# Attention with single-buffered v: each v load issued in two parts by partitions, and the next head's v asked for one step later

## The chip, the core and the metric

The kernel runs on one core of one Trainium2 chip. The time is the device time of one execution in microseconds (us), the median of three runs. TensorE (PE) multiplies, VectorE (DVE), ScalarE (ACT) and GpSimd (POOL) work element by element, SyncE (SP) issues the transfers (DMAs), which 16 DMA engines carry out.

## The reference, cut to what matters

One layer of an encoder runs over two sequences of 272 and 1040 tokens (16 of them are prepended). A gated feed-forward half-step, then a mixer of four differential attention heads beside a pooling branch, a projection, a second feed-forward half-step and a final norm. The part that the change touches is the attention of one head:

```python
logits = jnp.einsum('bqhcd,bkhcd->bhcqk', q_blk, k).astype(jnp.float32) * scale
logits = logits + bias[None, :, None]
p = jax.nn.softmax(logits, axis=-1)
a = p[:, :, 0] - lam * p[:, :, 1]
return jnp.einsum('bhqk,bkhd->bqhd', a.astype(v.dtype), v)
```

followed by a norm of each output row. All data are float32.

## The kernel before, in words

**Products.** Each float32 operand is split into a high and a low part, and a product is made of three (`mm3`, lines 157 to 163): high x high (L161), low x high (L162), high x low (L163). So v is held as two tiles, `vh` and `vl`, and a product with v first needs `vh` (L161), then `vl` (L162).

**v in memory.** The projection before the attention writes q, k and v to DRAM tensors (`q_d`, `k_d`, `v_d`). `load_v(hd, q)` (lines 817 to 830) reads one head's v of one sequence (`q` is 0 for the 272 tokens, 1 for the 1040). Tokens lie on partitions in groups of `TK` = 92 or 116. Per part (high, low) there are two loads: a main one of all full groups (L826; 2 groups on 92 partitions, 92 KB, or 8 groups on 116 partitions, 464 KB) and a tail (L828; 88 partitions, 44 KB, or 112 partitions, 56 KB). Each run of consecutive bytes is one row of 128 floats, 512 B. That is four issues per head and sequence, 32 in all. The tiles have one buffer each (`bufs=1`): the next head's v can be loaded only when the last product with the old one is done.

**Steps.** There are 40 steps, 10 for each head: 2 blocks of 128 query rows of the short sequence, then 8 of the long one. `run(i)` (lines 978 to 995) writes, in this order: the logits of step i for the first map (L845, L846, evicted with the bias by DVE at L848, exponentiated by ACT at L863), the combination of step i-1 (`combine`: L872 on DVE; L875 and L876 on POOL for the long sequence), the work of `early[i]`, the transposes of step i-`LAG` (`LAG` = 3; L893, evicted by ACT and DVE as `at`), the logits of the second map, further transposes, and the work of `late[i]`. Products with v (`av`) are in `early`, three groups at a time, so those of one pair of long query blocks are spread over three steps; their norm (L223 to L229, L924, L242) and the write of `o` (L938) are in `late`.

**Loads.** They are put into `late` by hand (lines 947 to 974): k, bias and v of the next head, and q of the next pair of blocks in each even step, two issues (L791). With `s0` the first long step of head hd and `end` the step after its last, v of the long sequence of head hd+1 is written at `end + LAG + 1`, in a step numbered 14, 24 or 34; the last products with the old v are in `early` of the step after it (15, 25, 35), the first with the new v in `early[17]`, `early[27]` and `early[37]`. Before step 2, `load_v(0, 0)` and `load_v(0, 1)` load head 0's.

**Order of the queues.** All DMAs of this kernel are issued from SP, in order: an issue that waits holds up all behind it. The order in which each engine's instructions stand is not just the written one. The framework's planner takes the written order as priority and its own estimate of when each instruction is ready, and places it in its engine's queue; the queues are fixed when the kernel is built.

After the attention, lines 1209 to 1248 project its output; the `cat` loads (L807) bring the written outputs of heads and pooling groups back.

Of the kernel before, what the change touches and what calls it, by code (L numbers as in the profile page):

```python
# [11 lines left out]
F32 = mybir.dt.float32  # L12
# [48 lines left out]
LAG = 3  # L61
# [41 lines left out]
def encoder(ctx: ExitStack, tc: tile.TileContext, a: dict):  # L103
    nc = tc.nc
# [525 lines left out]
    rows = [[row[:, s : s + NS] for s in pair] for pair in places]  # L630
# [186 lines left out]
    def load_v(hd, q):  # L817
        nt = len(KT[q])
        m = TK[q]
        s = LENS[0] * q  # L820
        vv = []
        for t in range(2):
            v = qp.tile([m, nt, P], F32R, tag=f"v{t}{q}", name="v", bufs=1)
            src = v_d[t][:, hd * P : (hd + 1) * P]
            full = (nt - 1) * m
            nc.sync.dma_start(out=v[:, : nt - 1].bitcast(F32), in_=src[s : s + full].rearrange("(j p) d -> p j d", p=m))  # L826
            tail = KT[q][-1][1]
            nc.sync.dma_start(out=v[:tail, nt - 1].bitcast(F32), in_=src[s + full : s + full + tail])  # L828
            vv.append(v)
        state["v", hd, q] = vv  # L830
# [112 lines left out]
    def at(i, fn, *args):  # L943
        late[i].append((fn, args))

    per = len(QT[0]) + len(QT[1])
    for hd in range(HEADS - 1):
        s0 = per * hd + len(QT[0])
        end = s0 + len(QT[1])
        k_pool = ("pre", "qp")[(hd + 1) % 2]  # L950
        at(s0 + 1, load_k, "pre", hd + 1, 0)
        at(s0 + 1, load_bias, "pre", hd + 1, 0)
        at(s0 + 2, load_k, k_pool, hd + 1, 1)
        at(s0 + 4, load_bias, ("pre", "mp")[(hd + 1) % 2], hd + 1, 1)
        at(s0 + LAG + 3, load_v, hd + 1, 0)
        at(end + LAG + 1, load_v, hd + 1, 1)
    for s_ in steps:
        i = s_["n"]
        if s_["i"] == 0 and s_["si"] + 1 < len(supers):
# [1 line left out]
        if s_["i"] == SUPER - 1:  # L961
            nt = len(KT[s_["q"]])
            j = i + LAG
# [195 lines left out]
    with st:  # L1159
        load_v(0, 0)  # L1160
        load_v(0, 1)
        i = len(W_IN_LAST)
        while i < last_step + LAG or any(k >= i for k in early) or any(k >= i for k in late):
            run(i)
            i += 1
# [17 lines left out]
    rows = {}  # L1183
# [27 lines left out]
    for b in PAIRS2[0]:  # L1211
        s = BS2[b][0]
# [16 lines left out]
    for i, pair in enumerate(PAIRS2):  # L1229
# [5 lines left out]
        for m0 in range(0, KC, 2):  # L1235
            ws = [split_unit(raws[m]) if i == 0 and m < 2 else wcols(w_out, m) for m in (m0, m0 + 1)]
            for b in pair:
                s = BS2[b][0]
# [161 lines left out]
```

## Time and profile before

| | |
|---|---|
| median of 3 runs | 2452.47 us (2451.22 to 2454.18) |
| the profiled execution, own time | 2450.31 us |
| its span, first to last instruction | 2448.5 us |
| mean granted PE clock over the span | 0.979 of full speed |
| PE busy | 2336.4 us, 95% |
| DVE busy | 1506.1 us, 62% |
| ACT busy | 803.8 us, 33% |
| POOL busy | 387.6 us, 16% |
| transferred | 264.67 MB, mean 108 GB/s |

How to read it: busy shares are means over the whole span, while the attention steps that the change touches fill some 230 us of it, from about 1190 to 1422 us. There, what an engine waited for is read from the waits and the timeline. Times in the rows count from the span's start. A row of a timeline gives start and duration in us, and in brackets the idle time before it and what ended that. The granted clock is a share of full speed: 1.00 is 2.4 GHz, 0.50 is 1.2 GHz.

### The profile page before, as it was taken

What the parts mean: (1) busy time and instruction counts of PE and PEld (TensorE: products, weight loads), DVE (VectorE), ACT (ScalarE), POOL (GpSimd) and SP (SyncE); (2) the same over time, 40 slices, a digit from 0 to 9 for tenths busy, and PEclk for the clock granted to TensorE, in tenths of its full rate; (3) what the DMA queues carried; (4) which work ended last, traced back from release to release, by engine and by line L of the source; (5) the groups of instructions that cost most, each with busy time, mean ns of one, the idle gap of its engine ahead of it and who ended that gap; (6) DMA issues with size and microseconds to landing.
All of it is one profiled execution on the core that took longest, in us unless ns stands there. A gap on an engine that the chain in (4) does not pass through costs nothing.

```text
span 2448.5 us, 38316 instructions
## 1 busy us (share of the span) xinstructions
PE 2336.4 (95%) x14578; PEld 2181.6 (89%) x14578; DVE 1506.1 (62%) x2834; ACT 803.8 (33%) x1705; POOL 387.6 (16%) x479
## 2 busy tenths in 40 slices
PE   5999999999999998999888898899999999999998
PEld 5899999999888887889778898889999999988886
DVE  7964545448676667344477747685455446667665
ACT  6533333335011123111377723453333334211113
POOL 0000000000111124111376743100000000021112
PEclk7999999999999999999999998999999999999999
DMA  8422222245232224545754154432122216323222
GB/s 234 118 80 72 65 64 75 70 150 174 77 96 79 82 71 134 167 145 159 186 134 124 49 166 154 133 96 74 57 80 73 74 57 222 116 82 96 86 69 86
DMA packets 294591, 264.67 MB, mean 108 GB/s; under 512 B 22048, under 2 KB 254072, under 8 KB 293896
## 3 DMA queue, kind: packets, MB, share of 16 engines
q1 hardware_dynamic: 294408, 262.24, 35.3%
q8 instruction: 114, 1.87, 0.3%
q14 instruction: 69, 0.57, 0.1%
HBM read 190.79 MB, written 75.61 MB: 109 GB/s over the span
## 4 chain that ended last, share of the span: by engine, by line
PE 82%; DVE 8%; DMA 4%; POOL 2%; issue 2%; ACT 1%; SPq 1%; POOLq 0%; ACTq 0%; DVEq 0%
PE bank L162 26%; PE bank L161 26%; PE bank L163 26%; DVE wl L152 1%; DMA v<-v_d 1%; PE bank L893 1%; PE pair L845 1%; PE pair L846 1%; PE bank L242 1%; DMA wraw<-in_ffn_w_up 1%; DMA wraw<-in_ffn_w_gate 1%; DMA cat<-cat_d 1%; POOL l L876 0%; POOL ry L223 0%; DVE h L328 0%
## 5 line engine op out<-in xcount | busy, mean ns | idle before, releaser
L152 DVE TENSOR_TENSOR wl<-wraw,wh 128x512 fp32r<-128x512 f32 x320 | 235.3, 740 | 296.1 <-ACT wh L146 219.8
L530 DVE SCALAR_TENSOR_TENSOR h<-bank,h 128x272 f32<-128x272 f32 (+2 forms) x528 | 313.1, 601 | 155.3 <-PE bank L163 151.3
L161 PE MATMUL bank<-hl,wh 128*128 128x512 f32 (+2 forms) x1056 | 380.4, 360 | 0.0
L162 PE MATMUL bank<-hl,wl 128*128 128x512 f32 (+2 forms) x1056 | 379.4, 359 | 0.0
L163 PE MATMUL bank<-hl,wh 128*128 128x512 f32 (+2 forms) x1056 | 379.1, 359 | 0.0
L146 ACT CAST hl<-hraw 128x272 fp32r<-128x272 f32 (+2 forms) x132 | 72.7, 552 | 517.2 <-PE bank L162 438.6
L155 POOL TENSOR_TENSOR hl<-hraw,hl 128x272 fp32r<-128x272 f32 (+1 forms) x44 | 34.7, 790 | 1239.9 <-ACT hl L146 1148.9
L163 PEld LDWEIGHTS bank<-hl,wh 128*128 128x128 f32 x1056 | 199.2, 189 | 31.6
L161 PEld LDWEIGHTS bank<-hl,wh 128*128 128x128 f32 x1056 | 199.2, 189 | 31.5
L162 PEld LDWEIGHTS bank<-hl,wl 128*128 128x128 f32 x1056 | 199.1, 189 | 31.4
L146 ACT CAST wh<-ws 128x512 fp32r<-128x512 f32 x224 | 138.4, 620 | 252.4 <-PE bank L163 156.0
L451 ACT COPY hid<-bank 128x324 f32<-128x324 f32 (+1 forms) x264 | 112.7, 427 | 279.5 <-PE bank L163 278.9
L152 DVE TENSOR_TENSOR wl<-ws,wh 128x512 fp32r<-128x512 f32 x224 | 153.7, 689 | 73.2 <-ACT wh L146 72.4
L149 POOL TENSOR_SCALAR wh<-wraw 128x512 fp32r<-128x512 f32 x152 | 115.1, 759 | 526.4 <-PE bank L163 245.2
L161 PE MATMUL bank<-t1h,wh 128*128 128x324 f32 (+1 forms) x352 | 110.3, 314 | 9.5 <-ACT wh L146 9.4
L162 PE MATMUL bank<-t1h,wl 128*128 128x324 f32 (+1 forms) x352 | 111.3, 316 | 4.0 <-DVE wl L152 3.9
L161 PE MATMUL bank<-t2h,wh 128*128 128x324 f32 (+1 forms) x352 | 110.2, 313 | 5.1 <-ACT hid L451 5.1
L162 PE MATMUL bank<-t4h,wl 128*128 128x324 f32 (+1 forms) x352 | 109.8, 312 | 3.1 <-DVE wl L152 3.0
L161 PE MATMUL bank<-t4h,wh 128*128 128x324 f32 (+1 forms) x352 | 109.4, 311 | 3.5 <-DVE hid L465 3.5
L161 PE MATMUL bank<-t3h,wh 128*128 128x324 f32 (+1 forms) x352 | 109.4, 311 | 1.8 <-ACT wh L146 1.8
L162 PE MATMUL bank<-t3h,wl 128*128 128x324 f32 (+1 forms) x352 | 109.7, 312 | 1.0 <-DVE wl L152 1.0
L161 PE MATMUL bank<-b21h,wh 128*128 128x324 f32 (+1 forms) x352 | 110.4, 314 | 0.3
(238 smaller groups left out, 6376.1 us busy)
## 6 DMA issues: line engine op xcount, KB each, us to landing
wraw<-in_ffn_w_gate SPq DMA_DIRECT2D x56, 512.0 KB
wraw<-in_ffn_w_up SPq DMA_DIRECT2D x56, 512.0 KB
hraw<-hid_d SPq DMA_DIRECT2D x88, 256.0 KB
wraw<-in_ffn_w_down SPq DMA_DIRECT2D x44, 512.0 KB
hid_d<-hid SPq DMA_DIRECT2D x88, 162.0 KB
hid_d<-hid SPq DMA_DIRECT2D x88, 160.0 KB
k<-k_d SPq DMA_DIRECT2D x32, 260.0 KB
h<-h_d SPq DMA_DIRECT2D x16, 512.0 KB
```

Of the source, the lines that this page charges most:

```text
L146: nc.scalar.copy(out=out, in_=in_)
L149: nc.gpsimd.tensor_scalar(out=out, in0=in_, scalar1=1.0, scalar2=1.0, op0=ALU.mult, op1=ALU.mult)
L152: nc.vector.tensor_sub(out, in_, hi.bitcast(F32))
L155: nc.gpsimd.tensor_sub(out, in_, hi.bitcast(F32))
L161: nc.tensor.matmul(out=ps, lhsT=wh, rhs=xh, start=first, stop=False, skip_group_check=on)
L162: nc.tensor.matmul(out=ps, lhsT=wl, rhs=xh, start=False, stop=False, skip_group_check=on)
L163: nc.tensor.matmul(out=ps, lhsT=wh, rhs=xl, start=False, stop=last, skip_group_check=on)
L242: nc.tensor.matmul(out=ps[:, j * m : (j + 1) * m], lhsT=r[:, j : j + 1].broadcast_to([m, P]), rhs=ident[:m, :m], start=True, stop=True,)
L451: nc.scalar.copy(out=to[s], in_=ps[s])
L530: nc.vector.scalar_tensor_tensor(out=h[b][:, m], in0=ps, scalar=0.5, in1=h[b][:, m], op0=ALU.mult, op1=ALU.add)
L845: nc.tensor.matmul(out=ps[:, m], lhsT=qs, rhs=kh[:, ks], start=True, stop=False)
L846: nc.tensor.matmul(out=ps[:, m], lhsT=qs, rhs=kl[:, ks], start=False, stop=True)
```

## The change

Each main load of v is issued in two parts by partitions: partitions 0 to 111 and 112 to 115 of the long sequence's, 0 to 79 and 80 to 91 of the short one's. The tails stay as they are. So a head has six v issues per sequence in place of four, 48 in all in place of 32. And the long sequence's v of the next head is written into the `late` work of the step after the one where it was (15, 25, 35 in place of 14, 24, 34), that is, behind the last products with the old v.

```diff
@@ load_v
             full = (nt - 1) * m
-            nc.sync.dma_start(out=v[:, : nt - 1].bitcast(F32), in_=src[s : s + full].rearrange("(j p) d -> p j d", p=m))
+            rows = src[s : s + full].rearrange("(j p) d -> p j d", p=m)
+            for p0, p1 in ((0, m - m % 16), (m - m % 16, m)):
+                nc.sync.dma_start(out=v[p0:p1, : nt - 1].bitcast(F32), in_=rows[p0:p1])
             tail = KT[q][-1][1]
@@ the loads put into late
         at(s0 + LAG + 3, load_v, hd + 1, 0)
-        at(end + LAG + 1, load_v, hd + 1, 1)
+        at(end + LAG + 2, load_v, hd + 1, 1)
```

## Rows read from the trace of the kernel before

**Rows 1.** The page's chain that ended last, by engine.

```profile
PE 82%; DVE 8%; DMA 4%; POOL 2%; issue 2%; ACT 1%; SPq 1%; POOLq 0%; ACTq 0%; DVEq 0%
```

**Rows 2.** Waits of PE, 1190 to 1425 us: total, times, longest.

```profile
PE bank L161 <- DMA v<-v_d: 14.2, 2, 7.2
PE pair L845 <- DMA q<-q_d: 9.6, 2, 8.8
```

**Rows 3.** PE's timeline, the long idle stretches of the attention stage.

```profile
1213.28 0.58 PE L162 MATMUL bank<-at,v 116*128 116x256 f32 x1 [4.47 <-DMA v<-v_d]
...
1273.71 0.56 PE L845 MATMUL pair<-k,q 128*128 128x260 f32 x1 [8.84 <-DMA q<-q_d]
...
1330.53 0.55 PE L161 MATMUL bank<-at,v 116*128 116x256 f32 x1 [6.99 <-DMA v<-v_d]
...
1385.96 0.55 PE L161 MATMUL bank<-at,v 116*128 116x256 f32 x1 [7.24 <-DMA v<-v_d]
```

**Rows 4.** The chain that ended last, in order of time: start, us, what.

```profile
541.62 5.94 DMA wraw<-in_ffn_w_up
...
1269.29 4.28 DMA q<-q_d
1314.42 15.97 DMA v<-v_d
```

**Rows 5.** SP's timeline of issues, heads 0 to 2.

```profile
1214.68 3.58 SPq L791 DMA_DIRECT2D q<-q_d  x4
...
1222.56 0.82 SPq L807 DMA_DIRECT2D cat<-cat_d  x2
...
1257.29 4.57 SPq L826 DMA_DIRECT2D v<-v_d  x2
1261.91 7.34 SPq L828 DMA_DIRECT2D v<-v_d  x2
1269.29 0.42 SPq L791 DMA_DIRECT2D q<-q_d  x1
...
1314.05 4.88 SPq L826 DMA_DIRECT2D v<-v_d  x2
```

**Rows 6.** Line 826: issues, ns of one (min/median/max), first and last start.

```profile
L826 SPq DMA_DIRECT2D v<-v_d x16: 254/316/4897, 1190.1 to 1370.1; - x16
```

**Rows 7.** Windows: us, busy per engine, PEclk, DMA share, GB/s; weights, then v.

```profile
541.00:547.00 6.00, 6.00 (x43) 6.00 (x42) 2.85 (x5) 2.10 (x5) 0.00 (x0) 1.00 1.09 364
...
1315.00:1320.00 5.00, 5.00 (x43) 4.91 (x42) 4.31 (x14) 4.91 (x12) 4.83 (x4) 1.00 0.26 71
```

**Rows 8.** PE's timeline, last product with head 1's v and the transposes after it.

```profile
1313.85 0.28 PE L163 MATMUL bank<-at,v 112*128 112x256 f32 x1
...
1316.52 0.60 PE L893 MATMUL bank<-ident,l 128*116 128x128 f32 x4
...
1321.59 0.62 PE L893 MATMUL bank<-ident,l 128*116 128x128 f32 x4
...
1322.78 0.76 PE L893 MATMUL bank<-ident,l 128*116 128x128 f32 x5
```

**Rows 9.** Windows of 10 us after the idle stretches at heads 1 to 3.

```profile
1273.70:1283.70 10.00, 9.99 (x67) 10.00 (x68) 6.54 (x19) 6.25 (x14) 1.83 (x2) 0.77 0.38 121
1330.50:1340.50 10.00, 9.97 (x62) 10.00 (x63) 5.40 (x15) 5.49 (x11) 3.50 (x3) 0.70 0.45 137
1386.00:1396.00 10.00, 10.00 (x66) 10.00 (x67) 5.84 (x17) 5.08 (x10) 3.61 (x2) 0.75 0.04 14
```

**Rows 10.** Windows: PE, PEld, DVE, ACT, POOL busy; idle to idle, and quiet.

```profile
1273.70:1330.50 56.80, 48.77 (x384) 47.49 (x385) 45.16 (x129) 40.01 (x99) 37.91 (x43) 0.92 0.47 130
...
1280.00:1310.00 30.00, 28.93 (x243) 28.33 (x242) 28.04 (x79) 24.70 (x61) 20.12 (x21) 1.00 0.53 137
```

**Rows 11.** POOL's and PE's timelines in head 0.

```profile
1213.60 2.40 POOL L876 TENSOR_TENSOR l<-l 128x1040 f32<-128x1040 f32 x1
...
1218.56 1.17 PE L893 MATMUL bank<-ident,l 128*116 128x128 f32 x9
```

## The prediction

> **What bounds it now.** I read the chain that ended last first. TensorE (PE) carries 82% of it, and transfers only 4% [rows 1]; the change touches loads, so the question is where in the attention stage PE waits for a load. The longest of PE's waits there for a load are v, 14.2 us in two places, and q, 9.6 us in two [rows 2]. PE's timeline places them and shows one more of v [rows 3]: 4.47 us among the first products with the long sequence's v in head 0, 8.84 us for q where head 1's v is loaded, 6.99 us and 7.24 us for v where heads 2 and 3 begin. The chain passes through the same places: 4.28 us of q, then 15.97 us of v at head 2 [rows 4].
>
> Why q is late is in SyncE's queue [rows 5]. At the start of head 1 the two main v loads are issued at 1257.29 and, with the two tails, hold the queue until 1269.25; the q load written behind them goes out at 1269.29, lands 4.28 us later, and PE starts at 1273.71. At head 2 PE waits for v itself: issued at 1314.05, landed 15.97 us after its issue had ended. In single issues the line of the main loads takes 0.316 us in the median and up to 4.897 us [rows 6]: a long issue here is the queue held up, not work.
>
> Why v takes so long is in the DMA share [rows 7]. With the v loads alone in flight it is 0.26 and 71 GB/s, the share of about 4 of the 16 engines (0.26 x 16 = 4.2). Two weight loads of the same row length (512 B), of 512 KB each on 128 partitions, with loads of h behind them, run at 1.09 and 364 GB/s, and the first has landed 5.94 us after its issue [rows 4, 7].
>
> The Trainium skill (DMA: Bandwidth & Descriptors, "Why a DMA increments its semaphore by 16 and not by 1") says that a transfer gets the largest number of engines up to 16 that divides the outermost size on both sides: 4 for 116 or 92 partitions, 16 for 112 or 80, 12 for 12. By that rule the share of 0.26 is 116's, the trace agrees, and the big part would get all 16.
>
> **Part 1, the split.** Each main load of 464 KB becomes 448 KB on 112 partitions and 16 KB on 4; the small one for the first sequence becomes 80 and 12 partitions. Bytes and rows stay. No split load is in the trace; its landing is bounded by 5.94 us (spread like the weight loads) and 15.97 us (as now). I take 5.94, since the bulk now has the weight loads' form (a multiple of 16 partitions, 512 B rows) and the two tiles, 2 x 520 KB with tails, are the same bytes as those two weight loads. The split adds 16 issues in the whole kernel, 16 x 0.316 = 5.1 us of SyncE's queue, 4 per boundary or 1.3 us. They are hidden as long as v is not late; without that cover they cost up to 1.3 us per boundary. I take nothing here and keep 1.3 for the range.
>
> **Part 2, the move.** For heads 1 to 3 the four (now six) issues of the long sequence's v are written one step later. They pass the two q issues of that step in SyncE's queue, and the products of the next step that last read the old v in PE's. POOL's queue holds nothing of them. The buffer is single, so the load cannot start before the last product with the old v: at head 2 that is 1313.85 + 0.28 = 1314.13 [rows 8], and the load was issued at 1314.05, at once. The move thus costs nothing if the planner still puts the issue at that moment, and at most one step, 1321.59 - 1316.52 = 5.07 us from one set of transposes to the next [rows 8]. The planner does move issues far ahead of where they are written: a cat load that belongs to the last head went out at 1222.56, in head 0 [rows 5]. PE first needs the new v after 1322.78 + 0.76 = 1323.54. At once: landed at 1314.1 + 5.9 = 1320.0, 3.5 us early. A whole step later: 1325.1, 1.5 us late, 2.8 with the extra issues. I take 1 us late per boundary, 3 in all. No instruction gets a new kind of wait. Behind the v issues that wait for the buffer stand the bias, an o write and the next q loads, none with a reader before the next step; the q of the step itself, behind v at head 1, now stands ahead of it.
>
> **Sum.** The three boundaries lose their idle time, 8.84 + 6.99 + 7.24 = 23.1 us. The idle also brings the clock down: in the 10 us after each idle stretch the granted clock is 0.77, 0.70 and 0.75, that is, partly at the lower of the two levels, while PE is busy for all 10 us [rows 9]. That is 2.3 + 3.0 + 2.5 = 7.8 us more. Not all of it comes back, since the other engines caught up meanwhile. From 1273.7 to 1330.5 VectorE (DVE) is busy 45.16 of 56.8 us; in the quiet 30 us from 1280 it is busy 28.04, or 93.5% [rows 10]. At that share the same work takes 48.3 us, a gain of 8.5 where 6.99 + 2.3 = 9.3 were lost. So 0.8 us stays at each boundary, 2.4 in all. In head 0 the bound from above is 4.47 us; from below, the transposes at 1218.56 need what POOL finished at 1213.60 + 2.40 = 1216.00 [rows 11], so only 2.5 us can come back before that point. I take 3.5, between the two, since q is issued earlier too (it waited until 1214.68 in the queue behind the same loads, [rows 5]).
>
> 3.5 + 23.1 + 7.8 - 2.4 - 3 = 29.0 us. The profiled execution took 2450.31 us (span 2448.5), so 2421.3; the median of the runs, 2452.47, lies 2.2 above it, so **2423.5 us**.
>
> **Rivals.**
> - *v a whole step late.* For: the move writes it a step later, and bias and q issues behind v went out in the written order. Against: the planner's freedom, above. Each boundary keeps 2.8 us idle and the clock loss: 23.1 - 8.4 - 2.4 + 3.5 = 15.8 gained, 2436.7 us.
> - *DVE or POOL takes over.* For: DVE goes from 80% to 93% of a head. Against: it ran 93.5% for 30 us with PE busy 28.93 of them [rows 10]. If half of each boundary's 8.5 us stayed: 3.5 + 3 x 4.3 = 16.4, 2436 us.
> - *The split does not spread the load, and the move remains* (slower). The landing stays at 16 us. With the load asked for 5.07 us later, heads 2 and 3 wait 5.07 longer each; at head 1, v lands at 1257.3 + 5.1 + 16 = 1278.4 where PE wants it near 1266 (just after its idle began at 1264.87), 12.4 idle for 8.84. Sum +13.7: 2466 us. It decides where the landing exceeds some 11 us, 16 less the step. For: nothing in the trace shows that the number of partitions is the cause. Against: the share of 0.26 beside 1.09 at the same row length; chance 0.06.
> - *The planner reorders.* New issues shift its estimates, and with them every engine's order in the attention stage; new gaps as large as the gain would leave 2452, no change. Nothing in the trace prices it; for it is only that the order is not the written one.
>
> The Trainium skill (DMA: Bandwidth & Descriptors, "Rules for kernel authors") says not to bother with two transfers to disjoint partitions, as they share the same 16 engines and serialize, and to use one. By that rule the split brings nothing and the third rival's 2466 us would follow; the share of 0.26 does not bear it out, as one transfer here does not use the 16.
>
> **Chances.** Forecast 0.63, v late 0.17, DVE or POOL 0.08, no spreading 0.06, reordering 0.06 (0.05 of it no change, 0.01 slower). About 0.2%, 4.9 us, is what a measurement of this kernel can tell from no change. Faster 0.63 + 0.17 + 0.08 = 0.88; same 0.05; slower 0.06 + 0.01 = 0.07. The range: all idle, all clock loss and head 0's 4.47 would be 35.4 us, 2417, with 3 us for the spread of the runs (2451.22 to 2454.18) 2414; upward it takes in the two rivals near 2436.5, with about the same for the spread 2439. The last two cases, 0.12, stay outside.
>
> **What would show it.** In the new trace: DMA share well over 0.5 while v loads; no single issue of the main loads near 4.9 us; a landing of about 6 us; q issued ahead of v at head 1; PE's waits for v and q in the stage down from 28 us to under 4; the clock at 1.00 where the idle was; the attention stage shorter by about 29 us, the rest of the span unchanged. It is wrong if v is still issued at the old moment but lands late, if PE shows new waits for POOL or DVE of several us at the same places, or if the time saved in the stage is lost after it.

## The result and the profile after

The changed kernel took 2422.63 us (median of 4 runs, 2420.77 to 2424.68) against 2451.84 us of the kernel before in the same comparison: ratio 0.9888, 95% interval 0.9876 to 0.9899. The forecast was 2423.5 us in 2414 to 2439. The span of the profiled execution fell from 2448.5 to 2422.1 us, by 26.4 us, where the medians differ by 29.2.

The chain that ended last, by engine, after (answers to [rows 1]):

```profile
PE 82%; DVE 9%; DMA 3%; POOL 2%; issue 2%; ACT 1%; SPq 0%; POOLq 0%; ACTq 0%; DVEq 0%
```

No load of q or v is left in it. PE's waits in the attention stage (us in total, times, longest), against [rows 2]:

```profile
PE bank L895 <- POOL l L878: 6.9, 5, 2.5
PE pair L847 <- DVE mx L850: 5.0, 13, 1.4
PE bank L242 <- POOL rr L229: 1.2, 1, 1.2
```

The waits for v and q are gone, all of them. Lines behind the change count two more than before: L893 is L895, L876 is L878, L845 is L847, L826 is L828 (one more again in experiments 3 and 10). What has grown is the wait for POOL, 6.9 us in five places. In the kernel before it was in two, and one of these, of 1.4 us, is there in both (at 1200.78 before, at 1203.30 after):

```profile
PE bank L893 <- POOL l L876: 2.3, 2, 1.4
```

PE's timeline after, at the other four places; these answer to [rows 3]:

```profile
1213.14 1.20 PE L895 MATMUL bank<-ident,l 128*116 128x128 f32 x9 [0.52 <-POOL l L878]
...
1218.57 1.75 PE L895 MATMUL bank<-ident,l 128*116 128x128 f32 x9 [2.48 <-POOL l L878]
...
1234.95 0.43 PE L895 MATMUL bank<-ident,l 128*116 128x128 f32 x2 [1.51 <-POOL l L878]
...
1239.87 0.43 PE L895 MATMUL bank<-ident,l 128*116 128x128 f32 x2 [0.95 <-POOL l L878]
```

All four lie in head 0, and what they mean is taken up at experiment 7. Where the kernel before had 8.84, 6.99 and 7.24 us of idle time, at the start of heads 1 to 3, there is nothing over 1.4 us. SyncE's issues at heads 1 and 2, against [rows 5]:

```profile
1258.40 1.00 SPq L791 DMA_DIRECT2D q<-q_d  x2
1261.47 0.82 SPq L828 DMA_DIRECT2D v<-v_d  x2
1262.34 0.31 SPq L830 DMA_DIRECT2D v<-v_d  x1
1262.70 0.93 SPq L828 DMA_DIRECT2D v<-v_d  x2
1263.67 0.32 SPq L830 DMA_DIRECT2D v<-v_d  x1
...
1306.99 0.82 SPq L828 DMA_DIRECT2D v<-v_d  x2
1307.87 0.49 SPq L830 DMA_DIRECT2D v<-v_d  x1
1308.40 3.56 SPq L828 DMA_DIRECT2D v<-v_d  x2
1312.00 0.32 SPq L830 DMA_DIRECT2D v<-v_d  x1
```

Both q loads go out ahead of v at head 1, and the six v issues take 1263.99 - 1261.47 = 2.5 us where four took 12.0; at head 2 they take 5.3 us. PE's timeline, the last products with the old v and the first with the new one (compare [rows 8]):

```profile
1261.16 0.28 PE L163 MATMUL bank<-at,v 112*128 112x256 f32 x1
...
1269.24 0.36 PE L161 MATMUL bank<-at,v 116*128 116x256 f32 x1
...
1306.68 0.28 PE L163 MATMUL bank<-at,v 112*128 112x256 f32 x1
...
1315.88 0.36 PE L161 MATMUL bank<-at,v 116*128 116x256 f32 x1
```

So v is issued 0.03 us after the old one comes free (1261.16 + 0.28 = 1261.44; 1306.96), although it is written a step later, and it is there without a wait 7.8 and 8.9 us after its first issue. The windows while v loads (PE, PEld, DVE, ACT, POOL busy, then granted clock, DMA share, GB/s), and one head from the first products with its v to the next head's, against [rows 7, 10]:

```profile
1261.50:1266.50 5.00, 5.00 (x43) 4.83 (x41) 4.29 (x14) 4.62 (x12) 4.83 (x4) 1.00 0.78 184
1307.00:1312.00 5.00, 5.00 (x43) 4.80 (x42) 4.28 (x13) 5.00 (x12) 4.66 (x7) 1.00 0.97 287
1269.20:1315.80 46.60, 45.75 (x377) 44.36 (x376) 43.08 (x127) 38.14 (x95) 37.41 (x43) 1.00 0.67 179
```

The share is 0.78 and 0.97 where it was 0.26. The granted clock is 1.00 in all three. The head takes 46.6 us between these marks; in the kernel before it took 54.9, from 1275.63 to 1330.53 (the 56.8 us of [rows 10] begin 1.9 us earlier, at the logits that waited for q). DVE is busy 43.08 of 46.60 us, 92%: near the 93.5% of the quiet stretch that the forecast used.

At head 3, where v's first issue is at 1354.25, no byte moves just before it, so that its load can be seen almost alone (a write of `o` and two q loads go out only from 1359.90 on):

```profile
1353.00:1354.50 1.50, 1.50 (x15) 1.50 (x14) 1.46 (x6) 1.39 (x4) 1.17 (x6) 1.00 0.00 0
1354.50:1360.50 6.00, 6.00 (x51) 5.78 (x50) 4.92 (x14) 5.65 (x14) 5.83 (x4) 1.00 0.81 178
```

6 us at 178 GB/s are 1.07 MB, as much as the two tiles hold (2 x 520 KB): the split load is through about 6 us after its first issue.

Measured from product to product (the last one with each head's long v), in one trace of each kernel, the stage divides like this:

| us | before | after | gained |
|---|---|---|---|
| first long logits to the end of head 0's v | 66.9 | 68.0 | -1.1 |
| head 1 | 56.3 | 45.5 | 10.8 |
| head 2 | 55.6 | 47.9 | 7.8 |
| head 3 | 48.4 | 38.6 | 9.8 |
| to the last norm (L242) | 3.9 | 3.9 | 0 |
| the stage | 231.2 | 203.9 | 27.3 |

The span gained 26.4: the stage began 2.5 us later in this execution (1193.2 for 1190.7), and what follows it took 1.6 us less. The first of these is no part of the change, as PE's order up to there is the same, and the stage began anywhere from 1189.3 to 1193.2 us in the profiled executions.

### The profile page after: what moved, and what is told of

It reads as the page before. It is cut to its first block, busy times and chain, and to the rows that moved or that the text cites. A ratio compares the mean times of both kernels' runs of the same rounds, so it can differ in the third digit from the quotient of the medians.

```text
span 2422.1 us, 38343 instructions
## 1 busy us (share of the span) xinstructions
PE 2330.8 (96%) x14578; PEld 2173.1 (90%) x14578; DVE 1505.1 (62%) x2834; ACT 804.4 (33%) x1705; POOL 389.5 (16%) x479
## 4 chain that ended last, share of the span: by engine, by line
PE 82%; DVE 9%; DMA 3%; POOL 2%; issue 2%; ACT 1%; SPq 0%; POOLq 0%; ACTq 0%; DVEq 0%
PE bank L162 26%; PE bank L161 26%; PE bank L163 26%; DVE wl L152 2%; PE pair L847 1%; PE bank L895 1%; PE pair L848 1%; DMA wraw<-in_ffn_w_gate 1%; DMA wraw<-in_ffn_w_up 1%; PE bank L242 1%; POOL l L878 1%; DVE ws L411 1%; DVE ws L414 0%; POOL ry L223 0%; DVE h L328 0%
## 5 line engine op out<-in xcount | busy, mean ns | idle before, releaser
L162 PE MATMUL bank<-b22h,wl 128*128 128x324 f32 (+1 forms) x352 | 109.3, 310 | 0.8 <-DVE wl L152 0.8
```

The source lines that it names most:

```text
L162: nc.tensor.matmul(out=ps, lhsT=wl, rhs=xh, start=False, stop=False, skip_group_check=on)
```

## The experiments

Three things were open: which of the two edits did it, whether the number of partitions is the cause or only the cut, and why head 0 gained nothing. All ratios are to the kernel before, timed beside it, with the 95% interval in brackets; times of heads and stages come from one trace of each kernel.

**1. The split alone.** In the changed kernel:

```diff
-        at(end + LAG + 2, load_v, hd + 1, 1)
+        at(end + LAG + 1, load_v, hd + 1, 1)
```

> The split alone; v of the long sequence is asked for where it was before. Theory (the split cures the wait: the load runs on more engines, so it lands in about 6 us and holds the issue queue about 4 us instead of 12): PE waits for v at heads 0, 2 and 3 gone; at head 1 both q issues stand behind six short v issues, so q is ready near 1266 against PE's need near 1265 and 0 to 2 us of the 8.84 us stay. Ratio to the kernel before 0.988 to 0.992. Rival (the move did it, the split is idle): waits of about 7 us for v at heads 2 and 3 and 8.8 us for q at head 1 stay, ratio 0.998 to 1.002.

Ratio 0.9909 (0.9894 to 0.9924), 2424.93 us. PE waits for neither v nor q. At head 1 both q issues do stand behind v, but not for long:

```profile
1257.10 1.43 SPq L828 DMA_DIRECT2D v<-v_d  x3
1258.58 0.32 SPq L830 DMA_DIRECT2D v<-v_d  x1
1258.94 0.36 SPq L828 DMA_DIRECT2D v<-v_d  x1
1259.35 0.32 SPq L830 DMA_DIRECT2D v<-v_d  x1
1259.71 0.90 SPq L791 DMA_DIRECT2D q<-q_d  x2
```

Six issues hold the queue for 2.6 us instead of 12. The stage takes 205.9 us for the changed kernel's 203.9, with the difference in head 1 (47.5 for 45.5). The split is nearly all of the gain: 23.6 us of medians (2448.56 to 2424.93), where the whole change, timed again in experiment 5, gains 23.9.

**2. The move alone.** In the kernel before, `LAG + 1` becomes `LAG + 2`.

> The move alone; each v load is one transfer again, on 116 and 92 partitions. Theory: the DMA share while v loads stays near 0.26 and the landing near 16 us; q at head 1 is issued ahead of v, so its 8.84 us go, but v is then late there (about 1257.3 + 16 = 1273 or later against a need near 1266, 7 to 12 us); heads 2 and 3 wait 7 to 12 us. Ratio 0.998 to 1.006. Rival (the move did it): waits for v under 2 us, ratio 0.988 to 0.992.

Ratio 0.9995 (0.9986 to 1.0004): no change. PE's waits, from the chain and from the timeline (first the chain's pieces, then PE):

```profile
1261.33 11.49 DMA v<-v_d
1312.08 15.76 DMA v<-v_d
```

```profile
1272.86 0.58 PE L162 MATMUL bank<-at,v 116*128 116x256 f32 x1 [7.35 <-DMA v<-v_d]
...
1327.97 0.55 PE L161 MATMUL bank<-at,v 116*128 116x256 f32 x1 [6.79 <-DMA v<-v_d]
...
1382.60 0.55 PE L161 MATMUL bank<-at,v 116*128 116x256 f32 x1 [7.28 <-DMA v<-v_d]
```

At head 1 the q loads now go ahead (1253.43), and PE's 8.84 us for q have turned into 7.35 for v: the first v issue is at 1256.48 and the last part lands at 1272.82, 16.3 us later. The DMA share from 1257 to 1262 is 0.24. This is a wait that takes the place of the one removed.

**3. Another cut.** As the changed kernel, but 115 and 1 partitions for the long sequence:

```diff
-            for p0, p1 in ((0, m - m % 16), (m - m % 16, m)):
+            cut = (80, 115)[q]
+            for p0, p1 in ((0, cut), (cut, m)):
```

> As the changed kernel, with the same number of issues in the same places, but the long sequence's main load cut into 115 and 1 partitions instead of 112 and 4. Theory (what counts is that the big part's partitions divide evenly among many engines; 115 has 5 as its largest divisor up to 16): DMA share while v loads about 0.31, landing 12 to 14 us, PE waits of 3 to 9 us for v at each of heads 1 to 3, ratio 0.994 to 1.002. Rival (any cut into two parts does it, or the extra issues and the new order): as the changed kernel, ratio 0.988 to 0.990.

Ratio 0.9971 (0.9962 to 0.9981), 2440.97 us. The chain's pieces and PE at head 1:

```profile
1260.53 3.52 SPq L829
1264.94 8.28 DMA v<-v_d
```

```profile
1273.36 0.55 PE L162 MATMUL bank<-at,v 116*128 116x256 f32 x1 [3.56 <-DMA v<-v_d]
...
1327.20 0.50 PE L162 MATMUL bank<-at,v 116*128 116x256 f32 x1 [3.52 <-DMA v<-v_d]
...
1377.70 0.35 PE L161 MATMUL bank<-at,v 116*128 116x256 f32 x1 [4.14 <-DMA v<-v_d]
```

The number of issues and their places are the changed kernel's, and yet each boundary waits 3.5 to 4.1 us. From the first v issue at 1260.20 the load lands at 1264.94 + 8.28 = 1273.22, after 13.0 us: four fifths of experiment 2's 16.3. At heads 2 and 3 it is 14.8 and 13.1 us, for experiment 2's 16.1 and 16.2; at head 2 a bias and two q loads had been issued just before. The DMA share while v loads, expected near 0.31:

```profile
1264.10:1269.10 5.00, 4.92 (x39) 4.33 (x37) 4.83 (x15) 4.34 (x13) 4.58 (x8) 1.00 0.39 103
```

In the same window of experiment 2 it is 0.29, with 74 GB/s. A cut into two does not do it; which cut decides.

The Trainium skill (DMA: Bandwidth & Descriptors, "Why a DMA increments its semaphore by 16 and not by 1") has a transfer run on as many engines as the largest number up to 16 that divides its outermost size; that is 5 for 115 partitions and 4 for 116. The landings at heads 1 and 3 agree (13.0 and 13.1 us for 16.3 and 16.2); the 14.8 us at head 2 lie above four fifths.

**4. No cut, but other groups.** In the kernel before, with the move:

```diff
-TK = (92, 116)
+TK = (96, 128)
-                    ap_.tile([116, cnt, SUPER * P], F32R, ...
+                    ap_.tile([128, cnt, SUPER * P], F32R, ...
```

> Not cut: token groups of 96 and 128 instead of 92 and 116, so that each main load is one transfer of a multiple of 16 partitions (the long one's tail 16, the short one's 80), with the move kept. The same number of groups, products and issues as before. Theory: v lands in about 6 us, no PE wait for v over 1 us, ratio 0.986 to 0.990. Rival (it is the cut, or the new order that 16 more issues bring): waits for v of 7 us and more stay, ratio 0.997 to 1.006.

Ratio 0.9902 (0.9889 to 0.9916), just above the expected 0.986 to 0.990, 2422.44 us, stage 204.5 us, and no wait for v or q. One transfer on 128 partitions does what the cut does, with the 32 issues of the kernel before. So neither the cut nor the extra issues are needed, only a number of partitions that spreads. Its main loads are those of the weight loads in [rows 7] in form.

**5. The changed kernel again**, on one chip with the next three.

> The changed kernel itself, unedited, on the same chip as the next three, so that they can be set against it. Ratio to the kernel before 0.987 to 0.990 as measured first; as the split alone (0.9909) if the move is worth nothing.

Ratio 0.9897 (0.988 to 0.9913), 2424.63 us. The intervals of this, of experiment 1 and of experiment 4 overlap: the times do not tell the move from none; the 2 us in head 1 are seen in traces alone. The gain is 23.9 us here for 29.2 in the first comparison, most of it because the kernel before was faster (2448.55 us for 2451.84).

**6. The move, one step more**: `end + LAG + 3`.

> The changed kernel with the long sequence's v written yet another step later (end + LAG + 3). Theory (the planner issues the load when the buffer comes free, so where it is written matters little, and the spread load lands with some us to spare): v issues within 1 us of where they are in the changed kernel, no PE wait for v over 1 us, ratio 0.987 to 0.991. Rival (a step written later is a step issued later): v issued about 5 us later and 1.5 to 3 us late at each of heads 1 to 3, PE waits for v of 5 to 9 us in all, ratio 0.991 to 0.995.

Ratio 0.9892 (0.9877 to 0.9906). Issues of v and PE at head 2:

```profile
1305.07 0.82 SPq L828 DMA_DIRECT2D v<-v_d  x2
...
1311.06 1.01 SPq L828 DMA_DIRECT2D v<-v_d  x2
```

```profile
1317.07 0.35 PE L162 MATMUL bank<-at,v 116*128 116x256 f32 x1 [0.22 <-DMA v<-v_d]
```

Half right. The high part goes out where it did (113.8 us after the first long logits in both), the low part 4.5 us later than in the changed kernel (119.7 for 115.2). PE starts on it 6.0 us after its issue, having waited 0.22 us. That is also a direct reading of a split load's landing: some 6 us, with q and the short v loads issued beside it, as at head 3 of the changed kernel.

**7. Head 0.** There PE works through one long row of products with v, without logits between them. Counted in the traces, it is 54 products in the changed kernel and in the split alone, 31 in the kernel before and in experiment 4 (the expectation below counts 61 and 38 in PE's queue as built). From the last logits before it to the first behind it 14.9 us pass in the kernel before (1207.20 to 1222.06), 15.8 in the changed kernel and 13.4 in experiment 4. Meanwhile POOL, which needs the logits' exponentials, runs dry (the kernel before, then the changed one):

```profile
1227.91 1.22 POOL L875 TENSOR_SCALAR l<-l,rs 128x1040 f32<-128x1040 f32 x1 [11.91 <-DVE rs L872]
...
1231.21 1.21 POOL L877 TENSOR_SCALAR l<-l,rs 128x1040 f32<-128x1040 f32 x1 [12.70 <-DVE rs L874]
```

The q loads that the next logits need stand in SyncE's queue behind eight k issues of head 1, which are written four steps later here, for head 1 alone:

```diff
-        at(s0 + 2, load_k, k_pool, hd + 1, 1)
+        at(s0 + 2 + (4 if hd == 0 else 0), load_k, k_pool, hd + 1, 1)
```

> The changed kernel with head 1's k of the long sequence written four steps later (steps 8 in place of 4), so that the q loads of head 0 stand ahead of most of those eight k issues. Theory (head 0 gained nothing because the planner, with 16 more issues, put all products of two blocks ahead of the next logits, 61 product rows without logits in PE's queue where the kernel before had 38, and PE then waits for POOL): the gap closes, PE's waits for POOL in head 0 fall from about 6 us to under 2, the time from the first long logits to the last product with head 0's v falls from 68 to 60 to 64 us, ratio 0.985 to 0.987. Rival (POOL's own work bounds head 0): that time stays at 66 to 68 us, ratio as the changed kernel.

Ratio 0.9868 (0.9853 to 0.9883), 2416.12 us. PE's waits of the stage:

```profile
PE pair L847 <- DVE mx L850: 4.7, 8, 1.1
PE bank L926 <- DVE at L152: 2.4, 1, 2.4
PE bank L895 <- POOL l L878: 1.4, 1, 1.4
```

The waits for POOL fell from 6.9 to 1.4 us, and the time to the end of head 0's v from 68.0 to 55.7 us, more than expected. Heads 1 to 3 gave back 5.3 us of it (47.0, 51.0 and 39.3 for 45.5, 47.9 and 38.6), how much of that is work that the new order only carries past the mark was not separated. The stage takes 196.9 us, 7 less. In head 0 PE now goes at most 3.4 us without logits, and POOL is idle at most 3.4 us at a time. Head 0 was not bound by POOL's work, but by the order.

**8. Both.** Experiment 4's groups and k two steps later for head 1.

> Groups of 96 and 128 tokens (no cut, 32 issues) with the move, and head 1's k of the long sequence written two steps later; its PE queue has no stretch of more than 12 product rows without logits in the long steps. Theory: as e4 but with head 0's POOL waits gone, ratio 0.985 to 0.988, faster than the changed kernel by 0.1 to 0.3%. Rival (POOL's work bounds head 0): as e4, 0.989 to 0.991.

Ratio 0.9866 (0.9852 to 0.9881), 2416.33 us, stage 198.1 us. Medians of 7 and 8 are 8.5 and 8.3 us below the changed kernel's on the same chip; their intervals and its just overlap (at 0.988), while the stage is 6 to 7 us shorter in the traces. These two are the fastest versions found, ahead of both kernels.

**9. Only the later k**, two steps, in the kernel before.

> The kernel before, uncut v loads, not moved, with only head 1's long k written two steps later; PE's queue then has no stretch of more than 12 product rows without logits in the long steps. Theory (two separate losses: the v loads on few engines, and in head 0 the order): PE's waits for v and q at heads 1 to 3 stay (8.8, 7.0, 7.2 us); in head 0 the v load still lands about 20 us after its first issue, so its 4.5 us wait for v stays or grows and only 0 to 5 us are won; ratio 0.997 to 1.001. Rival (the order in head 0 is worth its 8 us by itself): ratio 0.995 to 0.997.

Ratio 0.9978 (0.997 to 0.9987). PE's idle stretches:

```profile
1211.82 0.56 PE L845 MATMUL pair<-k,q 128*128 128x260 f32 x1 [5.71 <-DMA q<-q_d]
...
1268.41 0.55 PE L161 MATMUL bank<-at,v 116*128 116x256 f32 x1 [6.77 <-DMA v<-v_d]
...
1323.87 0.55 PE L161 MATMUL bank<-at,v 116*128 116x256 f32 x1 [6.77 <-DMA v<-v_d]
...
1378.45 0.55 PE L161 MATMUL bank<-at,v 116*128 116x256 f32 x1 [7.17 <-DMA v<-v_d]
```

The three boundaries still wait about 7 us each, now all for v: at head 1 q goes out ahead of it. In head 0 PE waits 5.71 us for q, which stands behind the slow v issues. More was won than the 0 to 5 us expected: the stage shrinks by 6.6 us (to 224.6), 4.0 of them in head 0 (62.9 for 66.9). This and the change's 27.3 us make 33.9, beside the 34.3 that experiment 7 gains on the kernel before: the two losses add up.

**10. Only the long loads cut.** The short one's 92 partitions stay one transfer:

```diff
+            cut = (m, m - m % 16)[q]
+            for p0, p1 in ((0, cut), (cut, m))[: 1 + q]:
```

> The changed kernel with only the long sequence's main loads cut (112 and 4); the short one's 92 partitions stay one transfer. Theory (no engine waited for the short v; only the long one's landing counts): no PE wait for v over 1 us, ratio 0.988 to 0.991. Rival (the short loads on 4 engines still hold up the queue and the long loads behind them): PE waits for v or q of 2 us or more at a boundary, ratio 0.992 to 0.995.

Ratio 0.99 (0.9884 to 0.9915), stage 204.6 us, one wait for v of 0.3 us and none for q. The cut at 80 brings nothing that can be measured.

## Why the prediction was right, and where two of its terms were not

**What v's load costs.** Right. The share of 0.26 fits four engines of 16, and v's landing, not its moment of issue, held PE. Experiments 1 and 2 part the edits, 3 and 4 the cut from the number of partitions. The third rival (no spreading, 2466 us) fell: the landing at head 1 went from 16.3 us (experiment 2) to under 7.8, and at head 3 it took about 6, for the 5.94 taken. DVE and POOL did not take over at heads 1 to 3: no wait of PE for them there is over 1.4 us.

The Trainium skill's advice beside that rival (DMA: Bandwidth & Descriptors, "Rules for kernel authors") is one transfer on 128 partitions rather than two to disjoint halves, since both halves run on all 16 engines anyway. It speaks of halves that spread and does not carry over to 116 partitions, as experiment 1 shows with 0.9909; experiment 4 agrees with it for 128, where one transfer does as well as the cut one.

**The split's price.** Right: the 16 issues are hidden. The forecast's 0.316 us each was 0.424 in the median of the main parts (L828), and no issue lasted 4.9 us, though one took 3.1. Their time in the queue shows nowhere: experiments 4 and 10, with 16 and 8 issues fewer, take as long as the changed kernel within the noise.

**The move.** That it costs nothing if the planner issues the load at the buffer's release was right to 0.03 us; the 1 us of lateness per boundary, 3 in all, was mis-sized: 0. In the traces the move even wins 2.0 us at head 1 (47.5 in experiment 1, 45.5), which the sum left out. The rival "a whole step late" did not occur, even in experiment 6 but for 0.22 us.

**Clock and the other engines.** Of 23.1 us idle and 7.8 us at the lower clock, 10.8 + 7.8 + 9.8 = 28.4 came back. 2.5 stayed, where 2.4 were expected from DVE's share; that it was DVE that kept them was not tested.

**Head 0.** This is the term that failed: "I take 3.5". It measured -1.1. Up to the transposes that the forecast named the lower bound was exact: they start 27.9 us after the first long logits before (1218.56 - 1190.68) and 25.4 after (1218.57 - 1193.19), 2.5 us sooner, and then wait 2.48 us for POOL in place of 4.47 for v. But the 2.5 us were lost again behind that point, and the extra for q's earlier issue was worth nothing: q went out at 1205.89 in place of 1214.68, yet the logits that use it stood behind the long row of products in PE's queue. The wait for v had lain inside that row. Without it PE waited there for POOL and then had 23 more products to work through: the next logits came 32.3 us after the first long ones, where they had come after 31.4.

The fourth rival, the planner's new order, came true here, in part. In experiment 4, whose row is as short as in the kernel before, the same wait is there:

```profile
1217.44 1.93 PE L893 MATMUL bank<-ident,l 128*128 128x128 f32 x9 [2.48 <-POOL l L876]
```

Its waits for POOL sum to 5.9 us, the next logits come after 29.9 us, and head 0 takes 66.2 us, 0.7 less than before. So the longer row accounts for some 1.8 us (68.0 for 66.2) of the 4.6 that the term was off, if the other tiling is worth nothing by itself. The rest, 2.8 us, stays with the order that the kernel before already had: experiments 7 to 9 show that another order lifts the loss, in the kernel before too. Which estimate of the planner's the extra issues tipped was not tried.

The two errors, 3 us too little and 4.6 too much, nearly cancel: 27.3 us in the stage for 29.0. The time was hit more closely than its parts, and that is luck; so is part of the 29.2 us between the medians, which were 23.9 when timed again.

## What to carry to other kernels

Before moving a late load, see how many engines carry it: here a DMA share near a quarter while it was alone in flight, with issues that lasted several microseconds, was the sign that the transfer's shape was the fault, and it also delayed what was queued behind it. Give it a number of partitions that spreads, by a cut or, with no more issues and the same time, by the tiling. Asking for this load a step later only traded one wait for another. And look at the heads that should have gained and did not: a wait that is removed may have hidden another one behind it, here a long row of products without logits.

## What the runs showed of the hardware that was not expected

A load's landing followed the number of partitions: 16.1 to 16.3 us with 116 (experiment 2), 13.0 to 14.8 with 115 and 1 (experiment 3), about 6 with 112 and 4. One partition less, in a second transfer, was worth a fifth at two of three heads. And a slow transfer is paid for twice: the single issues of the uncut loads lasted up to 4.9 us each, and those of the tails behind them up to 7.2, so that loads of q, quick in themselves (4.28 us), reached PE 8.84 us late.
